# GLU before the attention, the SSM branch product beside the last pair of heads: one decoder layer on Trainium2

## The chip, the cores and the metric

One NeuronCore of a Trainium2 chip. The metric is the device time of one execution in microseconds. Engines as the profile names them: PE (TensorE matmul), PEld (its weight loads), DVE (VectorE), ACT (ScalarE), POOL (GpSimd), SP (SyncE, which issues most DMAs).

## The reference

One layer on 1040 positions (16 meta tokens and 1024 tokens) of width 1024, in float32:

```
xn = RMSNorm(h)
[q | k | v | u | gate_a | gate_b] = xn @ W_in
a  = stick-breaking attention(q, k, v)       (8 heads x 64, strictly causal)
y  = gelu(S5 state space model(u))           (512 channels)
s  = y * sigmoid(y @ W_glu + b)
h += (sigmoid(gate_a) * (a @ W_pa) + sigmoid(gate_b) * (s @ W_pb)) @ W_o
h += hierarchical MoE(RMSNorm(h))            (32 experts, two per token)
```

W_glu is 512 x 512, W_pa and W_pb are 512 x 1024. The change concerns s and the merge of the two branches.

## The kernel before

Every float32 product is made of three matmuls: both factors are split into a high and a low part (`split`, L101 on ACT and L102 on DVE) and `mm3` (L134 to L136) adds high x high, high x low and low x high in PSUM. Weights come through `load_w` (L150): a 512 KB tile `wr`, split into `wh` and `wl`, two buffers of each.

The stages, in the order of the source:

- Norms; the projection u; the SSM in four blocks of 128 channels (`ssm`), whose output goes to memory, `y_d` (L647). Beside it run the gates: 32 products `gt` with a sigmoid (L180), stored to `gate_d` (L181). 21 of them are woven into the SSM, 3 (`MF`) stand before the projections of the first heads, 8 beside the attention.
- The attention, in four pairs of heads. `att_proj` makes q, k and v of a pair (`qs`, `kh`, `kl`, `V`), `att_pair` its scores (L770, L771), their sigmoids (L773, L774, ACT), a mask (L776, POOL), a running product (L779, DVE), a product (L780, POOL), transposes (L794) and value products (L807, L812). Pairs 0 to 2 run beside the projections of the next pair, and their output goes to `attn_d` (L821). Pairs 0 and 2 use the buffers `aq0`, pairs 1 and 3 `aq1`.
- Beside pair 3, GLU: eight loads of y (L660) through two buffers, split into `yh` and `yl`; then for each of four blocks of 128 outputs and two halves of the tokens (`q`) twelve matmuls, a sigmoid (L681), a product with y (L682) and the split into `sh` and `sl`, which stay on chip. After it the attention output of pairs 0 to 2 is loaded and split into `ah` and `al` (L299); pair 3 writes its part there itself.
- The branch stage: for each of eight blocks `m` of 128 outputs and each half, twelve matmuls of the SSM branch (into `qk`), twelve of the attention branch (into `mm`), the two gates loaded (L347, L348), two products (L349, L353), a sum on POOL (L354) and the splits into the tiles `m` and `ms`. Gate tiles have two buffers each. The split of W_o runs beside it.
- The output projection, the router, the experts.

Tiles have fixed numbers of buffers, and a pool opened later takes the room of those closed before. `weave(main, fill, a, b)` sets the order in the source: b steps of `fill` evenly among a steps of `main`. A scheduler then puts the instructions of each engine into the order in which they become ready by its own estimates, earlier source first; on the chip each engine and SP run that order strictly.

```
weave(pair, chain(gl, loads()), 16, 18)   # before: GLU and the attn loads beside pair 3
```

Of the kernel before, what the change touches and what calls it, by code (L numbers as in the profile page):

```python
# [12 lines left out]
F32 = mybir.dt.float32  # L13
# [30 lines left out]
CL = (0, 512), (512, 768), (768, 1024)  # L44
SF, MF, GP = 21, 3, (3, 3, 2)
MQ = tuple((n, {'m': 6, 'ms': 2}[n]) for n in ('m', 'm', 'ms', 'm'))
MR = 6
CH3 = ((0, 352), (352, 696), (696, 1040))
CHV = ((0, 272), (272, 656), (656, 1040))
# [7 lines left out]
def weave(main, fill, n_main, n_fill):  # L57

    done = 0
    for k in range(n_main):  # L60
        next(main, None)
        while done * n_main < (k + 1) * n_fill:
            next(fill, None)
            done += 1


def drain(*gens):
    for g in gens:
        for _ in g:
            pass  # L70
# [3 lines left out]
def tile_block(ctx, tc, i, out):  # L74
# [3 lines left out]
    def pool(c, name, bufs=1, side=None, **kw):  # L78
        return c.enter_context(tc.tile_pool(name=name, bufs=bufs, side=side, reuse_waits="tile", **kw))
# [9 lines left out]
    u_d = dr.tile([512, T, NCH], F32, name="u_d")  # L89
    y_d = dr.tile([512, T, 128], F32, name="y_d")  # L90
    attn_d = dr.tile([512, S], F32, name="attn_d")
    gate_d = dr.tile([2 * D, S], F32, name="gate_d")
    h2_d = dr.tile([S, D], F32, name="h2_d")
    hg_d = dr.tile([S, D], F32, name="hg_d")
# [4 lines left out]
    def split(h, l, src, heng=None, leng=None):  # L99

        a = (A if heng is None else heng).copy(h, src)  # L101
        return a.ins, (V if leng is None else leng).tensor_sub(l, src, _f(h)).ins  # L102
# [29 lines left out]
    def mm3(ps, wh, wl, xh, xl, first, last):  # L132

        nc.tensor.matmul(ps, lhsT=wh, rhs=xh, start=first, stop=False)  # L134
        nc.tensor.matmul(ps, lhsT=wh, rhs=xl, start=False, stop=False)  # L135
        nc.tensor.matmul(ps, lhsT=wl, rhs=xh, start=False, stop=last)  # L136


    with ExitStack() as ca:
# [21 lines left out]
        with ExitStack() as cx:  # L161
# [102 lines left out]
            nc.sync.dma_start(tab_d.rearrange("(a p) w -> p a w", p=128), ei[:, None, :].to_broadcast([128, 8, 128]))  # L264


            con = pool(ctx, "con2")
            c3 = ExitStack()
            ap = pool(c3, "att", bufs=2)
# [1 line left out]
            cq = ExitStack()  # L271
            aq[0] = pool(cq, "aq0", bufs=2)
            st = {}
            drain(islice(gen, MF), att_proj(tc, ap, aq[0], ps, proj, ident, 0, st))
            for hp in range(3):
                pair = att_pair(tc, ap, ps, ident, hp, st, attn_d)
                fill = chain(att_proj(tc, ap, aq[(hp + 1) % 2], ps, proj, ident, hp + 1, st), islice(gen, GP[hp]))
# [9 lines left out]
        with ExitStack() as c4:  # L287
            c5 = ExitStack()
            p = pool(c5, "br", side="right")
            ah, al, sh, sl = (p.tile([128, 4, S], F32R, name=n) for n in ("ah", "al", "sh", "sl"))  # L290
            with ExitStack() as c6:
                nc.sync.dma_start(gb, i["glu_b"])
                at = pool(c6, "glu", bufs=2, side="right")
                gl = glu(tc, at, ps, i, load_w, mm3, split, gb, y_d, sh, sl)

                def loads():
                    for k in range(3):
                        a = wp.tile([128, 2, 512], F32, name="wr", bufs=2)
                        nc.sync.dma_start(a, attn_d[k * 128:k * 128 + 128])  # L299
                        split(ah[:, k], al[:, k], a.rearrange("p a b -> p (a b)"))  # L300
                        yield
                dst += ah, al
                weave(pair, chain(gl, loads()), 16, 18)
                drain(pair, gl)
            c3.close()
            con3 = pool(ctx, "con3")
            mp = pool(ctx, "mp")

            M = [[mp.tile([128, 4, 512], F32R, name=n, bufs=b).rearrange("p a (b c) -> p (a b) c", b=2) for _ in range(2)]
                 for n, b in MQ]  # L310
            wop = [pool(ctx, "wo0"), None]
            wo = i["w_out"].rearrange("(k p) c -> p k c", p=128)
            W = [None, None]

            def load_wo(hf):
                W[hf] = []
                for q in range(4):
                    if hf:
                        hl = [wop[1].tile([128, 2, 512], F32R, name="w1", bufs=8) for _ in range(2)]
                    else:  # L320
                        if q % 2 == 0:
                            pg = [wop[0].tile([128, 4, 512], F32R, name="w", bufs=4) for _ in range(2)]
                        hl = [x[:, q % 2 * 2:q % 2 * 2 + 2] for x in pg]
                    W[hf] += [[x[:, k] for x in hl] for k in range(2)]
                    r = wp.tile([128, 2, 512], F32, name="wr", bufs=2)
                    nc.sync.dma_start(r, wo[:, 2 * q:2 * q + 2, hf * 512:hf * 512 + 512])
                    split(*hl, r)
                    yield

            wa = i["w_branch_attn"].rearrange("(k p) c -> p k c", p=128)  # L330
            wb = i["w_branch_ssm"].rearrange("(k p) c -> p k c", p=128)
            w0 = load_wo(0)
            p = pool(c5, "gat", side="right", bufs=2)
            for m in range(KD):
                h, l = load_w([wb[:, :, m * 128:m * 128 + 128], wa[:, :, m * 128:m * 128 + 128]])
                T2 = []
                for q in range(2):
                    c = slice(q * 512, q * 512 + 512)
                    t = ps.tile([128, 512], F32, name="qk", bufs=2)
                    for k in range(4):  # L340
                        mm3(t, h[:, k, :], l[:, k, :], sh[:, k, c], sl[:, k, c], k == 0, k == 3)
                    T2.append(t)
                for q in range(2):
                    c = slice(q * 512, q * 512 + 512)
                    ga = p.tile([128, 512], F32, name="ga")
                    gb = p.tile([128, 512], F32, name="gb")
                    nc.sync.dma_start(gb, gate_d[D + m * 128:D + m * 128 + 128, c])  # L347
                    nc.sync.dma_start(ga, gate_d[m * 128:m * 128 + 128, c])  # L348
                    V.tensor_mul(gb, gb, T2[q])  # L349
                    t = ps.tile([128, 512], F32, name="mm", bufs=2)  # L350
                    for k in range(4):
                        mm3(t, h[:, 4 + k, :], l[:, 4 + k, :], ah[:, k, c], al[:, k, c], k == 0, k == 3)
                    V.tensor_mul(ga, ga, t)  # L353
                    P.tensor_add(ga, ga, gb)  # L354
                    for r in range(2):
                        mh, ml = M[2 * q + r]
                        split(mh[:, m], ml[:, m], ga[:, r * 256:r * 256 + 256])
                if m >= 2:
                    next(w0, None)
            c5.close()  # L360

            wop[1] = pool(ctx, "wo1")
            drain(load_wo(1))
            cw.close()
            rp = pool(ctx, "raw", side="right")
            rt = out_proj(tc, c4, pool, ps, i, ident, M, W, h2_d, hg_d, tab_d, rstd, bcast, con, con3, ei)
# [281 lines left out]
                                        ap=[[S, CH], [CH * S, 8], [1, 128]]), Y[ti * CH:ti * CH + CH])  # L648


def glu(tc, p, ps, i, load_w, mm3, split, gb, y_d, sh, sl):
    nc = tc.nc
    V, A, P = nc.vector, nc.scalar, nc.gpsimd
    yh = p.tile([128, 4, S], F32R, name="yh", bufs=1)
    yl = p.tile([128, 4, S], F32R, name="yl", bufs=1)
    yd = y_d.rearrange("f t c -> f (t c)")

    def load(k, q):
        y = p.tile([128, 512], F32, name="y", bufs=2)
        nc.sync.dma_start(y, yd[k * 128:k * 128 + 128, q * 512:q * 512 + 512])  # L660
        return y

    for k in range(4):
        for q in range(2):
            c = slice(q * 512, q * 512 + 512)
            split(yh[:, k, c], yl[:, k, c], load(k, q))
    yield
    wg = i["glu_w"].rearrange("(k p) c -> p k c", p=128)
    for m in range(4):
        h, l = load_w([wg[:, :, m * 128:m * 128 + 128]])  # L670
        for q in range(2):

            y = p.tile([128, 512], F32, name="y", bufs=2).rearrange("p (t c) -> p t c", t=T)
            nc.sync.dma_start(y, y_d[m * 128:m * 128 + 128, :, q * 64:q * 64 + 64])
            t = ps.tile([128, 512], F32, name="mm", bufs=2)
            y4 = [x.rearrange("p k (t c) -> p k t c", t=T)[:, :, :, q * 64:q * 64 + 64] for x in (yh, yl)]
            for k in range(4):
                mm3(t, h[:, k, :], l[:, k, :], y4[0][:, k], y4[1][:, k], k == 0, k == 3)

            sg = p.tile([128, 64, T], F32, name="sg", bufs=1)  # L680
            A.activation(sg, t.rearrange("p (t c) -> p c t", t=T), AF.Sigmoid, bias=gb[:, m:m + 1])  # L681
            V.tensor_mul(sg, sg, y.rearrange("p t c -> p c t"))  # L682
            c = slice(q * 512, q * 512 + 512)
            split(sh[:, m, c], sl[:, m, c], sg.rearrange("p c t -> p (c t)"))
            yield


# [772 lines left out]
```

## Time and profile before

| | |
|---|---|
| runs | 1500.51, 1498.16, 1494.89 us; median 1498.16 |
| profiled execution | 1493.12 us, span 1491.1 us, mean granted clock 0.983 |
| busy share of the span | PE 95%, PEld 77%, DVE 72%, ACT 54%, POOL 29% |
| stages, us from the start | SSM to about 265; attention to 634; branch stage to 704; output projection and router to 840; experts after that |

A line of a group tells the line of the source, the engine, the operation, what is written and read, the shape, the count, and behind the bar the busy time, the mean duration in ns, and the idle time of the engine before it with what ended it. "<-" in brackets names who was waited for.

### The profile page before, as it was taken

The numbers are of one execution on the slowest core, as the hardware profiler recorded it, in microseconds if no ns is written. First come the engines' busy times: TensorE is split into PE (matmuls) and PEld (weight loads), VectorE is DVE, ScalarE is ACT, GpSimd is POOL, SyncE is SP. The second block draws the span as 40 slices with busy tenths as digits, with TensorE's granted clock in tenths as the row PEclk, the third lists the DMA queues.
The fourth block names the chain that finished last, engine by engine and source line by source line (L and its number), as shares of the span: only waits on it lengthen the run. The fifth ranks groups of instructions, "written<-read, shape, count | busy, mean of one in ns | idle before, by whom it ended". The sixth has DMA issues, their size and how long they took to land. (4 is left out here: it accounts for less than half of the span.)

```text
span 1491.1 us, 19767 instructions
## 1 busy us (share of the span) xinstructions
PE 1410.5 (95%) x7028; PEld 1144.0 (77%) x7028; DVE 1079.5 (72%) x1590; ACT 798.1 (54%) x1173; POOL 425.3 (29%) x372
## 2 busy tenths in 40 slices
PE   7989899999999979999999699999999999999994
PEld 5977788998989967778788477777777777777762
DVE  5799986465757577575476687777777777777757
ACT  6222222465656576431222277777777777777743
POOL 2162411134444464332255421111111111111033
PEclk9999999999999999999999799999999999999998
DMA  8233443211111114254863499999999999999753
GB/s 257 73 86 88 99 114 87 57 46 58 35 48 36 29 57 131 81 184 149 299 249 109 182 369 376 372 370 357 370 376 368 372 377 368 368 378 367 309 214 152
DMA packets 131749, 313.87 MB, mean 210 GB/s; under 512 B 27889, under 2 KB 81777, under 8 KB 107074
## 3 DMA queue, kind: packets, MB, share of 16 engines
q1 hardware_dynamic: 120450, 295.07, 55.3%
q0 software_dynamic: 9728, 16.83, 3.0%
q8 instruction: 56, 0.92, 0.2%
q10 hardware_dynamic: 1472, 0.69, 0.2%
q14 instruction: 43, 0.35, 0.1%
HBM read 284.03 MB, written 44.11 MB: 220 GB/s over the span
## 5 line engine op out<-in xcount | busy, mean ns | idle before, releaser
L136 PE MATMUL mm<-xh,wl 128*128 128x512 f32 (+4 forms) x608 | 220.3, 362 | 5.4 <-DVE wl L102 5.4
L134 PE MATMUL mm<-xh,wh 128*128 128x512 f32 (+4 forms) x608 | 220.7, 363 | 1.7 <-DVE kl L710 0.7
L135 PE MATMUL mm<-xl,wh 128*128 128x512 f32 (+4 forms) x608 | 220.1, 362 | 0.5 <-DVE xl L225 0.5
L136 PEld LDWEIGHTS mm<-xh,wl 128*128 128x128 f32 x608 | 114.5, 188 | 19.8 <-DVE wl L102 6.6
L134 PEld LDWEIGHTS mm<-xh,wh 128*128 128x128 f32 x608 | 114.2, 188 | 16.1 <-PE mm L136 1.6
L135 PEld LDWEIGHTS mm<-xl,wh 128*128 128x128 f32 x608 | 114.3, 188 | 13.5 <-DVE xl L225 1.0
L779 DVE TENSOR_TENSOR_SCAN pr<-pr 128x144 f32<-128x144 f32 (+3 forms) x64 | 91.2, 1426 | 42.1 <-POOL pr L776 40.8
L1174 POOL DMA_INDIRECT ye_d<-w,tab x32 | 33.3, 1041 | 270.9 <-ACT w L1167 270.3
L1090 DVE TENSOR_TENSOR w<-r,w 128x2048 fp32r<-128x2048 f32 x39 | 92.7, 2377 | 16.2 <-ACT w L1089 16.2
L1090 DVE TENSOR_TENSOR w<-m,w 128x2048 fp32r<-128x2048 f32 x40 | 90.8, 2284 | 16.7 <-ACT w L1089 16.7
L1096 POOL DMA_INDIRECT w<-hg_d,tab x31 | 40.7, 1314 | 207.1 <-PE tr L1117 205.8
L780 POOL TENSOR_TENSOR be<-be,pr 128x143 f32<-128x143 f32 (+3 forms) x64 | 86.7, 1359 | 38.9 <-DVE pr L779 36.6
L102 DVE TENSOR_TENSOR xl<-tr,xh 128x512 fp32r<-128x512 f32 x64 | 43.8, 686 | 57.9 <-ACT xh L101 57.9
L101 ACT CAST xh<-tr 128x512 fp32r<-128x512 f32 x64 | 37.5, 588 | 77.7 <-PE tr L1117 73.8
L102 DVE TENSOR_TENSOR wl<-wr,wh 128x1024 fp32r<-128x1024 f32 (+1 forms) x44 | 59.1, 1343 | 27.6 <-ACT wh L101 27.5
L1089 ACT CAST w<-r 128x2048 fp32r<-128x2048 f32 x40 | 76.3, 1908 | 3.8 <-PE mm L893 3.1
L1130 PE MATMUL a<-w,xh 128*128 128x512 f32 x196 | 77.8, 397 | 0.0
L101 ACT CAST wh<-wr 128x1024 fp32r<-128x1024 f32 (+1 forms) x44 | 44.5, 1011 | 61.8 <-PE mm L135 40.6
L1089 ACT CAST w<-m 128x2048 fp32r<-128x2048 f32 x40 | 76.5, 1912 | 0.8
L1132 PE MATMUL a<-w,xl 128*128 128x512 f32 x196 | 76.6, 391 | 0.0
L1131 PE MATMUL a<-w,xh 128*128 128x512 f32 x196 | 76.4, 390 | 0.0
L1167 ACT ACTIVATE w<-o,tab 128x512 f32<-128x512 f32 x64 | 44.2, 690 | 53.1 <-PE o L1160 53.1
(557 smaller groups left out, 3934.3 us busy)
## 6 DMA issues: line engine op xcount, KB each, us to landing
r<-in_w_dram SPq DMA_DIRECT2D x96, 1024.0 KB, 8.8
m<-in_w_dram SPq DMA_DIRECT2D x96, 1024.0 KB, 8.9
wr<-in_w_in_dram SPq DMA_DIRECT2D x32, 512.0 KB, 4.3
gate_d<-gt SPq DMA_DIRECT2D x32, 256.0 KB, 2.2
m<-ye_d SPq DMA_DIRECT2D x12, 512.0 KB, 8.6
x<-in_x_dram SPq DMA_DIRECT2D x8, 512.0 KB, 4.7
y<-y_d SPq DMA_DIRECT2D x16, 256.0 KB, 3.1
wr<-in_w_out_dram SPq DMA_DIRECT2D x8, 512.0 KB, 4.5
```

What stands on the lines that cost most here:

```text
L101: a = (A if heng is None else heng).copy(h, src)
L102: return a.ins, (V if leng is None else leng).tensor_sub(l, src, _f(h)).ins
L134: nc.tensor.matmul(ps, lhsT=wh, rhs=xh, start=first, stop=False)
L135: nc.tensor.matmul(ps, lhsT=wh, rhs=xl, start=False, stop=False)
L136: nc.tensor.matmul(ps, lhsT=wl, rhs=xh, start=False, stop=last)
L779: V.tensor_tensor_scan(rv, rv, rv, 1.0, op0=OP.mult, op1=OP.bypass)
L780: P.tensor_mul(be[:, :W - 1], be[:, :W - 1], pr[:, 1:W])
L1089: A.copy(h, raws[n])
L1090: low = lambda: (P if other else V).tensor_sub(l, raws[n], _f(h))
L1130: nc.tensor.matmul(acc[e][w], lhsT=xh[:, kk], rhs=h[:, k], start=(kk == 0), stop=False)
L1131: nc.tensor.matmul(acc[e][w], lhsT=xh[:, kk], rhs=l[:, k], start=False, stop=False)
L1132: nc.tensor.matmul(acc[e][w], lhsT=xl[:, kk], rhs=h[:, k], start=False, stop=(kk == KD - 1))
```

## The change

GLU becomes a stage of its own after the SSM, with the three `MF` gates after its first step (the loads and splits of y), and before the attention's buffers are opened. Its result goes to memory, `s_d`, and is not split there. Beside pair 3 a new generator `early` loads s and splits it, and makes for the first six (`AHEAD`) of the eight blocks m the SSM branch product, multiplies it with its gate and stores it over the gate in memory; after each of the first three blocks it loads a part of the attention output. The branch stage then has only the attention product for these six blocks and loads the finished SSM part in place of the gate; the last two blocks are as before. Branch weights of one matrix are now loaded for two blocks at a time.

```diff
+AHEAD = 6
+    s_d = dr.tile([512, S], F32, name="s_d")
...
+            with ExitStack() as c6:
+                nc.sync.dma_start(gb, i["glu_b"])
+                gl = glu(tc, pool(c6, "glu", bufs=2, side="right"), ps, i, load_w, mm3, split, gb, y_d, s_d)
+                next(gl)
+                drain(islice(gen, MF), gl)
+
             con = pool(ctx, "con2")
...
-            drain(islice(gen, MF), att_proj(tc, ap, aq[0], ps, proj, ident, 0, st))
+            drain(att_proj(tc, ap, aq[0], ps, proj, ident, 0, st))
...
             ah, al, sh, sl = (p.tile([128, 4, S], F32R, name=n) for n in ("ah", "al", "sh", "sl"))
-            with ExitStack() as c6:
-                nc.sync.dma_start(gb, i["glu_b"])
-                at = pool(c6, "glu", bufs=2, side="right")
-                gl = glu(tc, at, ps, i, load_w, mm3, split, gb, y_d, sh, sl)
-
-                def loads():
-                    for k in range(3):
-                        a = wp.tile([128, 2, 512], F32, name="wr", bufs=2)
-                        nc.sync.dma_start(a, attn_d[k * 128:k * 128 + 128])
-                        split(ah[:, k], al[:, k], a.rearrange("p a b -> p (a b)"))
-                        yield
-                dst += ah, al
-                weave(pair, chain(gl, loads()), 16, 18)
-                drain(pair, gl)
+            p = pool(c5, "gat", side="right", bufs=2)
+            wa, wb = (i[n].rearrange("(k p) c -> p k c", p=128) for n in ("w_branch_attn", "w_branch_ssm"))
+
+            def load_s(src, h, l, k):
+                a = wp.tile([128, 2, 512], F32, name="wr", bufs=2)
+                nc.sync.dma_start(a, src[k * 128:k * 128 + 128])
+                split(h[:, k], l[:, k], a.rearrange("p a b -> p (a b)"))
+
+            def branch(m, q, h, l, h_, l_, name):
+                c = slice(q * 512, q * 512 + 512)
+                t = ps.tile([128, 512], F32, name=name, bufs=2)
+                for k in range(4):
+                    mm3(t, h[:, k], l[:, k], h_[:, k, c], l_[:, k, c], k == 0, k == 3)
+                return t
+
+            def gate(row, m, q):
+                g = p.tile([128, 512], F32, name="ga" if row else "gb")
+                d = gate_d[row * D + m * 128:row * D + m * 128 + 128, q * 512:q * 512 + 512]
+                nc.sync.dma_start(g, d)
+                return g, d
+
+            def early():
+                for k in range(4):
+                    load_s(s_d, sh, sl, k)
+                yield
+                for m in range(AHEAD):
+                    if m % 2 == 0:
+                        w = load_w([wb[:, :, (m + n) * 128:(m + n) * 128 + 128] for n in range(2)])
+                    for q in range(2):
+                        g, d = gate(1, m, q)
+                        V.tensor_mul(g, g, branch(m, q, *(x[:, m % 2 * 4:m % 2 * 4 + 4] for x in w), sh, sl, "mm"))
+                        nc.sync.dma_start(d, g)
                         yield
+                    if m < 3:
+                        load_s(attn_d, ah, al, m)
+
+            dst += ah, al
+            fill = early()
+            weave(pair, fill, 14, 1 + 2 * AHEAD)
+            drain(pair, fill)
...
             for m in range(KD):
-                h, l = load_w([wb[:, :, m * 128:m * 128 + 128], wa[:, :, m * 128:m * 128 + 128]])
-                T2 = []
+                if m >= AHEAD:
+                    w = load_w([x[:, :, m * 128:m * 128 + 128] for x in (wb, wa)])
+                    at = 4
+                    T2 = [branch(m, q, *(x[:, :4] for x in w), sh, sl, "qk") for q in range(2)]
+                else:
+                    at = m % 2 * 4
+                    if not at:
+                        w = load_w([wa[:, :, (m + n) * 128:(m + n) * 128 + 128] for n in range(2)])
                 for q in range(2):
...
+                    (g_, _), (ga, _) = gate(1, m, q), gate(0, m, q)
+                    if m >= AHEAD:
+                        V.tensor_mul(g_, g_, T2[q])
+                    V.tensor_mul(ga, ga, branch(m, q, *(x[:, at:at + 4] for x in w), ah, al, "mm"))
+                    P.tensor_add(ga, ga, g_)
...
-def glu(tc, p, ps, i, load_w, mm3, split, gb, y_d, sh, sl):
+def glu(tc, p, ps, i, load_w, mm3, split, gb, y_d, s_d):
...
-            sg = p.tile([128, 64, T], F32, name="sg", bufs=1)
+            sg = p.tile([128, 64, T], F32, name="sg", bufs=2)
             A.activation(sg, t.rearrange("p (t c) -> p c t", t=T), AF.Sigmoid, bias=gb[:, m:m + 1])
             V.tensor_mul(sg, sg, y.rearrange("p t c -> p c t"))
-            c = slice(q * 512, q * 512 + 512)
-            split(sh[:, m, c], sl[:, m, c], sg.rearrange("p c t -> p (c t)"))
+            nc.sync.dma_start(s_d[m * 128:m * 128 + 128, q * 512:q * 512 + 512], sg.rearrange("p c t -> p (c t)"))
```

## Rows read from the trace of the kernel before

**Rows 1.** The page, busy us, share of the span, instructions.

```profile
PE 1410.5 (95%) x7028; PEld 1144.0 (77%) x7028; DVE 1079.5 (72%) x1590; ACT 798.1 (54%) x1173; POOL 425.3 (29%) x372
```

**Rows 2.** Timeline of PE, 258.5 to 266: start, duration, instruction.

```profile
259.02 0.39 PE L136 MATMUL mm<-xh,wl 128*128 128x512 f32 x1
...
265.27 0.39 PE L136 MATMUL mm<-xh,wl 128*128 128x512 f32 x1
```

**Rows 3.** Timeline of PE, 544.9 to 549.

```profile
545.79 0.28 PE L812 MATMUL pv<-wth,V 128*128 128x256 f32 x1
545.91 0.28 PE L812 MATMUL pv<-wtl,V 128*128 128x256 f32 x1
...
546.14 0.31 PE L812 MATMUL pv<-wtl,V 128*128 128x128 f32 x1
```

**Rows 4.** Groups of PE instructions, 520 to 704.

```profile
L134 PE MATMUL qk<-sh,wh 128*128 128x512 f32 x64 | 25.3, 395 | 1.6 <-DVE gb L349 1.6
L134 PE MATMUL mm<-ah,wh 128*128 128x512 f32 x60 | 23.8, 397 | 2.1 <-ACT sg L681 0.9 <-DVE ga L353 0.8 <-ACT ah L825 0.5
...
L807 PE MATMUL pv<-wth,V 128*128 128x256 f32 (+1 forms) x96 | 22.5, 366 | 0.9 <-DVE ao L820 0.5 <-ACT wth L801 0.4
L794 PE MATMUL tr<-ident,be 128*128 128x128 f32 x127 | 22.4, 291 | 1.9 <-POOL be L780 1.8
L770 PE MATMUL qk<-kh,qs 128*128 128x392 f32 (+8 forms) x36 | 14.1, 394 | 1.2 <-ACT be L774 1.0
...
L134 PE MATMUL mm<-yh,wh 128*128 128x512 f32 x32 | 12.9, 425 | 0.5 <-ACT yh L101 0.5
...
L812 PE MATMUL pv<-wtl,V 128*128 128x256 f32 (+1 forms) x24 | 6.8, 309 | 2.8 <-DVE wtl L804 2.8
```

**Rows 5.** Windows: length, busy us of PE, PEld, DVE, ACT, POOL, granted clock, DMA share, GB/s.

```profile
520.00:545.00 25.00, 19.26 (x122) 16.29 (x120) 17.40 (x22) 16.91 (x42) 18.25 (x21) 0.93 0.18 52
520.00:704.00 184.00, 168.21 (x822) 137.83 (x821) 121.56 (x144) 89.64 (x196) 76.56 (x74) 0.98 0.40 122
```

**Rows 6.** GLU's y loads and splits: ns min/median/max, first and last start; landing us.

```profile
L660 SPq DMA_DIRECT2D y<-y_d x8: 319/320/537, 538.7 to 568.2; - x8
...
DMA to landing us min/median/max: 2.7/2.8/3.1
...
L101 ACT CAST yh<-y x8: 617/620/674, 548.3 to 571.2; 128x512 fp32r<-128x512 f32 x8
L102 DVE TENSOR_TENSOR yl<-y,yh x8: 659/806/2445, 550.9 to 571.8; 128x512 fp32r<-128x512 f32 x8
```

**Rows 7.** Line 180 up to 262 us.

```profile
L180 ACT ACTIVATE gt<-mm x24: 585/594/605, 79.5 to 258.8; 128x512 f32<-128x512 f32 x24
```

**Rows 8.** Line 647, stores of y, and their landing.

```profile
L647 SPq DMA_DIRECT2D y_d<-Y x32: 303/432/1443, 166.0 to 264.7; - x32
...
DMA to landing us min/median/max: 1.9/2.4/4.1
```

**Rows 9.** Windows, an idle stretch in the SSM stage.

```profile
100.00:120.00 20.00, 12.40 (x53) 9.15 (x52) 19.83 (x11) 3.77 (x6) 10.86 (x4) 0.83 0.17 53
```

**Rows 10.** GLU's product with y, by its tile.

```profile
L682 DVE TENSOR_TENSOR sg<-sg,y x8: 1067/1096/1622, 574.5 to 608.3; 128x512 f32<-128x512 f32 x8
```

**Rows 11.** Waits, 240 to 300: waiting line, releaser, us in total, times, longest.

```profile
POOL V L729 <- DMA y_d<-Y: 16.3, 1, 16.3
```

**Rows 12.** Timeline of all engines, 684.2 to 692, one gate buffer; landing of line 348.

```profile
684.30 0.68 DVE L353 TENSOR_TENSOR ga<-ga,mm 128x512 f32<-128x512 f32 x1
...
685.15 1.29 POOL L354 TENSOR_TENSOR ga<-ga,gb 128x512 f32<-128x512 f32 x1 [4.47 <-DVE ga L353]
...
687.85 0.42 DVE L102 TENSOR_TENSOR m<-ga,m 128x256 fp32r<-128x256 f32 x1
...
688.30 0.32 SPq L348 DMA_DIRECT2D ga<-gate_d  x1
...
DMA to landing us min/median/max: 2.7/3.6/6.0
```

More of the change, by code (lines that the diff above doesn't have):

```diff
@@ L328, in load_wo @@
                     yield
-            wa = i["w_branch_attn"].rearrange("(k p) c -> p k c", p=128)
-            wb = i["w_branch_ssm"].rearrange("(k p) c -> p k c", p=128)
             w0 = load_wo(0)
-            p = pool(c5, "gat", side="right", bufs=2)
             for m in range(KD):
-                h, l = load_w([wb[:, :, m * 128:m * 128 + 128], wa[:, :, m * 128:m * 128 + 128]])
-                T2 = []
-                for q in range(2):
-                    c = slice(q * 512, q * 512 + 512)
[L339 to L354, printed above, removed]
+                if m >= AHEAD:
[6 more added lines that the diff above has]
+                        w = load_w([wa[:, :, (m + n) * 128:(m + n) * 128 + 128] for n in range(2)])
+                for q in range(2):
+                    (g_, _), (ga, _) = gate(1, m, q), gate(0, m, q)
[3 more added lines that the diff above has]
+                    P.tensor_add(ga, ga, g_)
                     for r in range(2):
@@ L678, in glu @@
                 mm3(t, h[:, k, :], l[:, k, :], y4[0][:, k], y4[1][:, k], k == 0, k == 3)
-            sg = p.tile([128, 64, T], F32, name="sg", bufs=1)
+            sg = p.tile([128, 64, T], F32, name="sg", bufs=2)
             A.activation(sg, t.rearrange("p (t c) -> p c t", t=T), AF.Sigmoid, bias=gb[:, m:m + 1])
             V.tensor_mul(sg, sg, y.rearrange("p t c -> p c t"))
-            c = slice(q * 512, q * 512 + 512)
-            split(sh[:, m, c], sl[:, m, c], sg.rearrange("p c t -> p (c t)"))
+            nc.sync.dma_start(s_d[m * 128:m * 128 + 128, q * 512:q * 512 + 512], sg.rearrange("p c t -> p (c t)"))
             yield
```

## The prediction, made before the changed kernel was run

> **What bounds the kernel now.** I read the page first: PE is busy 1410.5 of 1491.1 us [rows 1], so every matmul counts wherever it is put, and the change keeps their number. A move can only change the time in which PE has nothing to issue. So I looked for that time where the change acts: the windows view and the groups of PE's instructions for 520 to 704 us, from the last projections to the end of the branch products.
>
> Busy time misleads there. Matmuls overlap: one of 512 columns is listed with 0.39 us, but from 259.02 to 265.27 PE starts 27 of them, 0.23 apart [rows 2], and the 256-column products of attention start 0.12 apart [rows 3]. I therefore count. In 520 to 704 there are 64 lots of three for the SSM branch (192), 179 for the attention branch, 96 for GLU and 9 of projections: 476 by 0.2315 is 110.2 us [rows 4]. The transposes (127, and 3 of the projections) and the value products (96 and twice 24) are 274 by 0.12, 32 us. The score products, 36 and as many of the low part, lie between 0.12 and 0.23 by width; 72 by 0.16 is 11.5 us [rows 4]. Work is 154 of 184 us: 30 us without issue. The busy column would say 184 - 168 = 16 [rows 5]. The Trainium skill's "Perfetto Trace Analysis", section "Identifying the Most-Contended Engine", says that matmul busy time is no good measure because matmuls are pipelined; by the busy column the stretch could give back 16 us at most and the sum below would come out at least 12 us higher, while the starts in this trace side with the page.
>
> Of the 30 us, about 9 lie in 520 to 545 (122 short matmuls by some 0.13 is 16 of 25 us [rows 5]), most of the rest up to 640: pair 3 has only GLU beside it, and GLU's inputs come late. Its y loads go out from 538.7 and its first copy runs at 548.3 [rows 6].
>
> **The change, part by part.** *GLU moved ahead of the attention.* Its 96 matmuls (22.2 us) leave the late stretch and go between the last SSM output and pair 0's projections. What covers it there? The three gate products beside it in the source are no cover: all 24 gate tiles given out up to this point are done by 258.8 already, inside the SSM stage [rows 7]. In the kernel before, pair 0's projections follow at once (the products of 259.02 to 265.27 [rows 2]). After the change GLU needs y of the last block: its stores are issued until 264.7 and land 2.4 later, at 267 [rows 8]. Then eight y tiles go through two buffers: load 2.8, copy 0.62, subtraction 0.66 [rows 6], some 0.3 of hand-over, 4.4 us a pair. Three rounds and a last one with its second tile, 4.7: 267 + 13.2 + 4.7 = 285. In between only the first two steps can run three of their four parts (18 matmuls, 4.2 us). The other 78 take 18.0 us: 303.
>
> Two smaller costs come on top. The clock: in 100 to 120, where PE was busy 12.4 of 20 us, the granted clock averages 0.83: some 7 us at 1.2 GHz in place of 2.4, 0.17 x 20 = 3.4 us lost [rows 9]. GLU follows a gap, so I put 2 us into it (0 to 3.4). And each result waits for its second y load, its product with y (1.1 us [rows 10]) and now a store, through two buffers; 1 to 3 us at the start, I take 1. PE leaves GLU at about 306 (304 to 310). Pair 0's projections begin there instead of at 258.5, where the last gates end: 47.5 us later (45 to 52), 22.2 of them moved work and 25 new idle time.
>
> Can those projections run beside GLU instead? I think not. V of pair 0 shares its room with the SSM's last output: its clearing waited 16.3 us for the y store [rows 11]. GLU shares its room with the projections of the even pairs: y lay in memory from 541.5, the first copy into yh ran only at 548.3 [rows 6], after the last value product of pair 2 at 546.14 [rows 3]. In the change GLU's pool lies in this stretch again, so pair 0's projections would have to wait until GLU has read yh. The same rows make me expect that its y loads for the first three blocks do not go ahead of the last block's store.
>
> *Branch product beside pair 3.* 144 matmuls (33.3 us) replace GLU's 96 there. Their inputs lie in memory long before; sh and sl take the room of xh and xl, free after the last projection at about 521, not that of pair 2. Four loads of 512 KB, their splits and a weight block give a start near 540 to 546, so the 9 us of 520 to 545 stay. From there 33 us of branch and about 28 of pair 3 (the 44 us of attention counted above less the 16 done by 545) fill some 65 us; I leave 4 idle (2 to 14, since a product that waits for its PSUM tile holds pair 3's scores behind it on PE), and 2 at the seam.
>
> New on SP: 8 stores of s, 4 loads of it, and for 12 products a gate load and a store, each waiting for its DVE product, with the next gate load, the attn loads and the next weights behind it on SP. Twelve rounds through two buffers of load 3.6, product 0.7 [rows 12] and a store, at 2.4 like that of y [rows 8], are 40 us, inside pair 3's 65: no cost; without that cover they would cost 40 - 33 = 7. Splits are the same elements, only later. The extra 10 MB or so of transfers I cost at nothing: the DMA engines are busy 0.40 of 520 to 704 [rows 5].
>
> *Branch stage.* For m under 6 only the attention half is left, 12 matmuls a half row: 2.8 us. Its gate buffer is held from the product at 684.30 over POOL's addition and the last split to the reload at 688.30, 4.0, and the load lands 3.6 after [rows 12]: 7.6 for two buffers, 3.8 a half row. Before, 24 matmuls (5.6 us) hid that; now DVE's input is late by 1.0 twelve times, 12 us, less the first loads, which are early: I take 9 (0 if they run ahead, 14 if SP delays them).
>
> **Sum.** Late stretch: 154 - 22.2 + 9 + 4 + 2 + 9 = 156 instead of 184, 28 less. Early: 47.5 more. **+19 us**. With the bounds: from 45 - 40 = +5 (idle 9, 2, 0, 1) to 52 - 12 = +40 (idle 9, 14, 3, 14). The profiled execution took 1493.12, 5.0 less than the median of the runs, 1498.16; I set the 19 on the median: **1517**.
>
> **Rivals.** *GLU is covered* (ends on the other side). If pair 0's projections, 11 us for q and as much or more for k and v, do run in the gap of 258.5 to 285, GLU costs its 22.2 us of work alone: 22.2 - 28 = -6, and -18 at the low end of the late idle time; 1480 to 1492, faster from the point where over 20 of the 25 us are filled. For it: those products need nothing of GLU and took no pause before. Against it: the shared room. 0.18, two thirds of it faster by over 0.5%.
>
> *The y loads run early.* If the loads of blocks 0 to 2 do not wait for Y's room, only two tiles are left at 267, and GLU starts in full at 272 instead of 285: +6, 1504. 0.12. The Trainium skill's "DMA: Bandwidth & Descriptors", section "Measured (HBM→SBUF, 128 partitions, SWDGE, issued from GpSimd)", lists 341 GB/s at 1 MB; an estimate by it puts all 2 MB of y at 6 us, and the sum at +7. The rows show 2.8 us for 256 KB and two buffers, so here the ring sets the pace and not the rate.
>
> *The change does not do what it says.* If the loads of s and the branch weights sit on SP behind attn stores that wait for pair 2, or the gate ring holds PE, the product is not beside pair 3 but after it: the late idle time stays near 30 and the price is 47.5 - 22.2 = +25 to +33, 1523 to 1531. 0.15.
>
> **How the numbers follow.** The forecast, +5 to +40 with +19 likeliest, has 0.55; covered GLU 0.18; early y 0.12; no filling 0.15. Half a percent is 7.5 us, about what a measurement of this kernel can tell from no change. Faster: two thirds of 0.18, 0.12. Same: the rest of it, two thirds of early y and a twentieth from the forecast's low end, 0.18. Slower: 0.70. The range leaves out most of the covered case and the far end: 1497 to 1534.
>
> **What would show it.** Right: PE without work, but for a few GLU products, from about 259 to 285 with the granted clock at half; the first qs copy near 310 instead of 263.6; y loads in pairs 4.4 apart after the last y store; branch products of sh from about 540 between pair 3's products; gate reloads 3.8 apart in the branch stage. Wrong: projection products between 259 and 300 beside GLU's, or y loads before 260, or a late stretch with over 30 us idle.

## The result and the profile after

The changed kernel takes 1534.2 us, median of four runs (1531.05 to 1535.93), against 1497.85 for the kernel before beside them: ratio 1.0238, interval 1.0224 to 1.0253. That is 36 us slower; forecast were 19, with 1497 to 1534 as the range, so the time lies at its far end. The two profiled executions that are compared below lie 41 us apart, since the one of the kernel before was 5 us faster than its median.

The page of the changed kernel, busy time by engine, answers to [rows 1]:

```profile
PE 1424.7 (93%) x7028; PEld 1153.0 (75%) x7028; DVE 1078.5 (70%) x1586; ACT 798.8 (52%) x1169; POOL 420.4 (27%) x372
```

Again 7028 matmuls: the 41.2 us by which the profiled span grew (1491.1 to 1532.3) are time in which PE had nothing to issue, or ran at half clock (granted clock 0.76 and 0.73 in the first two windows below). The windows of the changed kernel (columns as in [rows 5]), the GLU stage first, then from the last projection to pair 3's last output and from there to the first output product:

```profile
255.00:270.00 15.00, 3.29 (x15) 2.32 (x13) 3.98 (x8) 4.10 (x7) 0.00 (x0) 0.76 0.38 105
270.00:285.00 15.00, 9.42 (x24) 5.50 (x24) 4.71 (x8) 3.94 (x7) 0.00 (x0) 0.73 0.37 115
285.00:310.00 25.00, 24.51 (x103) 19.44 (x102) 12.54 (x13) 8.99 (x13) 0.04 (x1) 0.97 0.89 236
...
567.50:682.20 114.70, 99.50 (x521) 85.83 (x519) 65.95 (x68) 60.08 (x136) 54.97 (x60) 0.93 0.39 127
682.20:746.10 63.90, 52.05 (x208) 40.13 (x209) 35.05 (x54) 17.16 (x36) 19.64 (x14) 0.95 0.51 169
```

The same two late stretches of the kernel before:

```profile
522.20:633.80 111.60, 98.88 (x521) 81.72 (x520) 76.56 (x79) 68.55 (x155) 55.70 (x60) 0.97 0.31 90
633.80:707.00 73.20, 70.14 (x303) 56.67 (x304) 45.49 (x66) 20.36 (x40) 21.65 (x14) 1.00 0.52 169
```

Fifteen matmuls in the first window, 24 in the second, 103 in the third: PE stands empty for y, then half empty. The stretch beside pair 3 holds 521 matmuls before and after, and is 3 us longer instead of shorter. The lots of three there, by the groups of PE's instructions in these two stretches, before and then after:

```profile
L134 PE MATMUL mm<-yh,wh 128*128 128x512 f32 x32 | 12.9, 425 | 0.5 <-ACT yh L101 0.5
...
L134 PE MATMUL qk<-sh,wh 128*128 128x512 f32 x16 | 6.5, 406 | 0.0
```

```profile
L136 PE MATMUL mm<-sh,wh 128*128 128x512 f32 x48 | 18.9, 395 | 0.0
```

The kernel before already ran 48 products of the SSM branch (16 by 3) beside the end of pair 3, besides GLU's 96. So the 144 early products do not put more work there than stood there; they replace these 144. The prediction counted GLU's 96 alone. The branch stage has lost 95 matmuls and only 9.3 us. The first `qs` copy came at 309.07 (263.6 before), the last projection at 567.5 (522.2): 45.3 us later. The late stretch is 178.6 instead of 184.8, 6.2 back; what follows it is 2.1 longer. 45.3 - 6.2 + 2.1 = 41.2.

Because busy time misleads for PE, I split each stretch into work and idle time: every matmul is charged the distance to the next start that its kind keeps while PE waits for nothing (0.227 us for 512 columns, 0.118 for 256, 0.108 for a transpose, the score products by their width), and the rest, half clock included, is idle. One kind keeps another distance: pair 3's value products of 256 columns, which take `wth` unsplit, one product in place of two, start 0.215 apart. Eight of them without a wait, before and then after (the last one's own 0.38 us leaves 1.51 for seven distances):

```profile
611.79 1.89 PE L807 MATMUL pv<-wth,V 128*128 128x256 f32 x8
```

```profile
663.87 1.89 PE L831 MATMUL pv<-wth,V 128*128 128x256 f32 x8
```

Pair 3 has 96 of these products (16 of them with 128 columns). Charged like the value products of the other pairs they would count 8.4 us too few, and those would look like idle time.

| us: length = work + idle | last projection to pair 3's last output | from there to the output projection | both |
|---|---|---|---|
| before | 111.6 = 90.3 + 21.7 | 73.2 = 68.8 + 4.0 | 184.8 |
| after | 114.7 = 90.3 + 24.8 | 63.9 = 47.2 + 16.5 | 178.6 |

(The rest of a few tenths is rounding and the matmul at the cut.) Predicted for both: 132 of work and 24 idle, 156 us. Work is 137.5; idle time is 41.3. The late stretch is 23 us longer than predicted: 5.5 of work and 17 of idle time. Half clock is a small part of it: beside pair 3 the granted clock is 0.93, which makes some 16 us at 1.2 GHz, and PE issued about 6 us of work in them, so that they cost some 6 us (some 3 in the kernel before, at 0.97).

### The profile page after: what moved, and what is told of

Read it like the earlier page. It is cut to its first block, busy times and chain, and to the rows that moved or that the text cites. A ratio compares the mean times of both kernels' runs of the same rounds, so it can differ in the third digit from the quotient of the medians.

```text
span 1532.3 us, 19824 instructions
## 1 busy us (share of the span) xinstructions
PE 1424.7 (93%) x7028; PEld 1153.0 (75%) x7028; DVE 1078.5 (70%) x1586; ACT 798.8 (52%) x1169; POOL 420.4 (27%) x372
## 5 line engine op out<-in xcount | busy, mean ns | idle before, releaser
L136 PEld LDWEIGHTS mm<-xh,wh 128*128 128x128 f32 x608 | 114.4, 188 | 16.4 <-PE mm L138 1.7
L104 DVE TENSOR_TENSOR wl<-wr,wh 128x1024 fp32r<-128x1024 f32 (+1 forms) x44 | 55.1, 1253 | 33.7 <-ACT wh L103 33.4
L797 ACT ACTIVATE pr<-qk 128x144 f32<-128x144 f32 (+6 forms) x112 | 52.1, 465 | 42.5 <-PE qk L795 28.0
```

## The experiments

### What is the GLU stage's price, and can it be covered?

**Eight y buffers**, in both places where `glu` makes `y`:

```diff
-        y = p.tile([128, 512], F32, name="y", bufs=2)
+        y = p.tile([128, 512], F32, name="y", bufs=8)
```

> GLU's y tiles have eight buffers in place of two; six of them lie beside the SSM's last output buffer, not in it. Theory (the gap in front of GLU is the two-buffer ring that starts only after the last y store): loads of blocks 0 to 2 go out before 265, GLU runs in full from about 271 in place of 284, and the time falls by 10 to 13: 1521 to 1524. Rival (the wait for the last block alone sets GLU's start; the ring is hidden behind it): under 4 us, 1530 to 1536.

Measured: 1527.17 us, ratio 1.021 (1.0193 to 1.0227), faster than the changed kernel by 4 us by the ratios and 7 by the medians, between the theory's 1521 to 1524 and the rival's 1530 to 1536. The y loads by their line, of the changed kernel:

```profile
L685 SPq DMA_DIRECT2D y<-y_d x8: 319/320/427, 266.0 to 279.2; - x8
...
DMA to landing us min/median/max: 2.8/2.8/3.0
```

and with eight buffers:

```profile
L685 SPq DMA_DIRECT2D y<-y_d x8: 338/428/433, 264.4 to 268.8; - x8
...
DMA to landing us min/median/max: 2.8/2.8/2.8
```

Each load lands after 2.8 us either way. With two buffers the eight go out over 13.2 us, with eight over 4.4, and `qs` starts 4.8 earlier (304.3). So the ring (the two buffers used in turn) costs 4 to 7 us, and the rest stays: no load went out before 264.4, when the last y stores had been issued, though the theory had those of blocks 0 to 2 ahead of them.

**Gates as cover.** Three of the gate products that stand beside pairs 0 to 2 are put behind `next(gl)`:

```diff
-SF, MF, GP = 21, 3, (3, 3, 2)
+SF, MF, GP = 21, 6, (2, 2, 1)
```

> Three of the gate products that run beside pairs 0 to 2 stand in the GLU stage instead (MF 6, GP 2,2,1): 3 x 24 matmuls x 0.2315 = 16.7 us of PE work, put into the 13 us in which PE waits for y. Theory (PE is the limit beside pairs 0 to 2, where the changed kernel idles 7.6 us in 259, so work taken out there shortens it one for one, and the GLU stage's wait hides it): GLU starts about 4 later, the last projection ends about 13 earlier, 1518 to 1525 us. Rival (the pairs need these products as cover for their own chain of scores, scans and transposes): the pairs idle that much more and the time stays at 1530 to 1536.

Measured: 1539.89, ratio 1.0266 (1.0242 to 1.029), 4 us slower than the changed kernel by the ratios, whose intervals overlap. The theory's 1518 to 1525 fell; the rival's reason held, though the time lies above its 1530 to 1536. The wait of PE for y in the GLU stage, in the changed kernel and then with the gates moved (engine, line, who was waited for: total us, times, longest):

```profile
PE mm L136 <- ACT yh L103: 17.3, 4, 11.7
```

```profile
PE mm L136 <- ACT yh L103: 3.5, 2, 2.1
```

PE's waits from 310 to 570, with the gates moved (the first 9 us are still GLU stage):

```profile
PE mm L136 <- ACT wh L103: 2.6, 4, 0.9
PE mm L138 <- DVE wl L104: 2.5, 4, 0.7
PE mm L136 <- DVE kl L734: 2.0, 2, 1.2
PE mm L136 <- DVE qs L725: 1.6, 2, 1.0
```

and of the changed kernel:

```profile
PE mm L138 <- DVE wl L104: 0.8, 2, 0.5
PE mm L136 <- DVE kl L734: 0.7, 1, 0.7
PE tr L756 <- ACT vf L744: 0.6, 1, 0.6
PE mm L136 <- DVE qs L725: 0.5, 1, 0.5
```

The cover is real: the GLU stage's idle time falls from 23.6 to 16.5. But beside pairs 0 to 2 idle time rises from 7.6 to 20.7, some 8 of these 13 us in many small waits for split weights and for evictions of the projections. So work could not be taken out of this stretch one for one, though 97% of it was work. The waits point to what the gate products had hidden there, the weight splits and the evictions; that is not shown apart from the order, since `weave` spreads fewer steps with fewer gates, and some 40 attention matmuls slid behind the last projection.

### Are the early branch products worth anything?

**No early products.** All eight blocks as in the kernel before; GLU stays early, s and the attention output are loaded beside pair 3.

```diff
-AHEAD = 6
+AHEAD = 0
...
+                for m in range(3):
+                    load_s(attn_d, ah, al, m)
+                    yield
...
-                    if m < 3:
-                        load_s(attn_d, ah, al, m)
...
-            weave(pair, fill, 14, 1 + 2 * AHEAD)
+            weave(pair, fill, 14, 4)
```

> GLU stays a stage of its own, but no branch product is made beside pair 3 (AHEAD 0); all eight blocks make theirs in the branch stage, as in the kernel before. Theory (the early products take away what covered the end of pair 3, and their gate ring stretches pair 3): pair 3 runs bare, some 60 us in place of the 83 between its first and last running product after the change, its end is again covered by SSM branch products, and the kernel is 10 to 25 us faster than after the change: 1510 to 1524. Rival (the early products do fill idle time of PE, and the whole loss is the gap in front of GLU): without them 144 matmuls of 0.23, 33 us, lose their cover: 1555 to 1567.

Measured: 1526.79, ratio 1.0202 (1.0183 to 1.022). Without them the kernel is 5 to 7 us faster, just above the theory's 1510 to 1524 and far from the rival's 1555 to 1567. Both stretches answer (windows of this run, cut as above):

```profile
568.40:667.80 99.40, 82.46 (x425) 69.38 (x423) 56.79 (x56) 56.56 (x132) 50.52 (x60) 0.88 0.21 67
667.80:741.00 73.20, 70.21 (x304) 56.70 (x305) 45.41 (x66) 20.44 (x41) 21.69 (x15) 1.00 0.54 169
```

Pair 3 ends after 99.4 us; with 96 matmuls more beside it (21.8 us: the 144 early ones, less the 48 of the SSM branch that stand beside its end without them) it takes 114.7, 15.3 more. In the branch stage the same products cost 73.2 - 63.9 = 9.3.

### Where does the branch stage idle?

Three runs. **W_o later** (`next(w0, None)` from m = 4 instead of 2) and **the two whole blocks first**:

```diff
-                if m >= 2:
+                if m >= 4:
```

> The first load of W_o goes out with branch block 4 in place of block 2. After the change SP stood from 667.8 to 685.7 before a branch weight load, because both weight tiles held parts of W_o whose split waited for pair 3's end at 682; the gate loads stood behind it. Theory (PE's restart after pair 3 waits on that queue): PE's idle time of 680 to 710, some 15 us, falls by 5 to 12: 1522 to 1529. Rival (the restart waits on the attention output alone): no change, 1531 to 1536.

```diff
-            for m in range(KD):
+            for n_m, m in enumerate((6, 7, 0, 1, 2, 3, 4, 5)):
...
-                if m >= 2:
+                if n_m >= 2:
```

> The branch stage takes blocks 6 and 7, whose SSM products are not made early, first. Theory (the end of pair 3 stands bare because no product without attention is left): 48 matmuls of 0.23, 11 us, run beside the last steps of pair 3, in the 22 us in which PE was idle between 663 and 700: 6 to 11 us faster than after the change, 1523 to 1528. Rival (those weights sit on SP behind waiting loads as well, or pair 3's steps are what PE waits for in any order): under 3 us, 1531 to 1536.

Measured: 1534.47 (1.0252, 1.0235 to 1.0269) and 1533.24 (1.025, 1.023 to 1.0269), both no change. The first did not do what it was made for. SP's own instructions in the changed kernel at the seam, where PE starts again after pair 3's last output:

```profile
667.52 0.32 SPq L317 DMA_DIRECT2D ga<-gate_d  x1
685.67 0.38 SPq L152 DMA_DIRECT2D wr<-in_w_branch_attn_dram  x1
...
687.90 0.38 SPq L360 DMA_DIRECT2D wr<-in_w_out_dram  x1
688.33 0.94 SPq L317 DMA_DIRECT2D gb<-gate_d  x2
```

and with W_o later:

```profile
657.66 0.43 SPq L360 DMA_DIRECT2D wr<-in_w_out_dram  x1
659.84 11.55 SPq L317 DMA_DIRECT2D ga<-gate_d  x2
689.74 0.38 SPq L360 DMA_DIRECT2D wr<-in_w_out_dram  x1
691.17 0.32 SPq L317 DMA_DIRECT2D gb<-gate_d  x1
```

SP stands from 667.8 to 685.7 in the one, from 671.4 to 689.7 in the other, before a load that needs a `wr` buffer, and the gate loads queue behind it: only the load that waits was exchanged. The order of blocks moved some 5 us of idle time from pair 3's end into the branch stage: pair 3's stretch takes 6.1 us more for 10.7 more of work. So these two leave the seam itself open.

**Four gate buffers:**

```diff
-            p = pool(c5, "gat", side="right", bufs=2)
+            p = pool(c5, "gat", side="right", bufs=4)
```

> Four buffers for each gate tile instead of two, nothing else. Theory A (the chain from gate load to freed buffer is longer than two steps of the product, both beside pair 3, 4.3 us a step against 2.8 of work, and in the branch stage): the idle time of the branch stage falls from 15 to about 5, pair 3 ends up to 4 earlier, 1519 to 1527 us. Theory B (the restart after pair 3 waits for the weight load behind the W_o parts, and the rest of pair 3 is its own chain): at most 3 gained, 1531 to 1535.

Measured: 1526.99, ratio 1.0189 (1.0167 to 1.0211), 7 us faster than the changed kernel. The waits of PE in the branch stage, of the changed kernel and then of this run:

```profile
PE mm L136 <- DVE gb L378: 11.1, 5, 7.0
```

```profile
PE mm L136 <- DVE gb L378: 5.8, 2, 5.5
```

The five waits for a gate become two, and the stretch 53.5 us instead of 63.9, with 2.3 less work in it. What is left is one long wait, 5.5 at the seam. But pair 3's stretch is no shorter (116.2): the gate ring was the price in the branch stage, not beside pair 3.

### Is pair 2's tail the cause?

In the changed kernel the splits of s stand in pair 2's last steps. POOL's products there, by its timeline:

```profile
576.26 6.04 POOL L804 TENSOR_TENSOR be<-be,pr 128x783 f32<-128x783 f32 x2
...
587.89 4.94 POOL L804 TENSOR_TENSOR be<-be,pr 128x1039 f32<-128x1039 f32 x2 [3.62 <-DVE pr L803]
```

The kernel before has the last of these lines at 537.04 with 2.55 us. **Order:** the splits of s, weights and attention output are queued behind the first step of pair 3, by its last sigmoid `a0` and its last running product `v0`:

```diff
-                for k in range(4):
-                    load_s(s_d, sh, sl, k)
+                a0, v0 = st["a"], st["v"]
+                with tc.issue_after(a0), tc.issue_after(v0):
+                    for k in range(4):
+                        load_s(s_d, sh, sl, k)
...
```

> The splits of s, of the first branch weights and of the attention output are queued, on ACT and on VectorE, behind the first step of pair 3 (its last sigmoid and its last running product), where the kernel before had the splits of y. Nothing else changes. Theory (these splits stand in pair 2's tail: between the last projection and pair 2's last POOL product there are 25 us against 17 in the kernel before, with the POOL products at 2.8 to 4.5 us instead of 1.6 to 2.2): pair 2 and the head of pair 3 are 5 to 9 shorter, and since pair 3 is set by its own chain the end moves by most of it: 1525 to 1530 us. Rival (the early products then start later by as much and the gate ring after them sets the end): pair 3's first output comes earlier, its last does not, 1532 to 1536.

Measured: 1531.33, ratio 1.0236 (1.0222 to 1.0251): no change. The same products in this run:

```profile
574.62 1.57 POOL L808 TENSOR_TENSOR be<-be,pr 128x783 f32<-128x783 f32 x1
...
578.74 1.80 POOL L808 TENSOR_TENSOR be<-be,pr 128x911 f32<-128x911 f32 x1 [2.06 <-DVE pr L807]
...
583.52 2.55 POOL L808 TENSOR_TENSOR be<-be,pr 128x1039 f32<-128x1039 f32 x2
```

The mechanism was there and went (pair 2's last long product starts 14.6 us after the last projection instead of 20.4), and the time did not follow: the splits now stand in pair 3's head, whose first output comes 38.7 after the last projection, as before the edit (38.6). My theory of this run fell, and the rival's sign, an earlier first output, did not come either.

### What does a product beside pair 3 cost?

Two runs with order and eight y buffers: with early products and four gate buffers, and without early products. The first is the changed kernel with the order above and

```diff
-            p = pool(c5, "gat", side="right", bufs=2)
+            p = pool(c5, "gat", side="right", bufs=4)
...
-        y = p.tile([128, 512], F32, name="y", bufs=2)
+        y = p.tile([128, 512], F32, name="y", bufs=8)
```

> The order of the splits, four buffers for each gate tile (7 faster alone) and eight y buffers (7 faster alone) together. Theory (three costs in three stretches): 1534 - 7 - 7 - 7 = 1513, 1510 to 1517 us; the stretch from the last projection to the output projection then is some 162 against 185 before and 179 after. Rival (order and gate buffers free the same time, since pair 3's chain limits both): 1518 to 1522.

Measured: 1519.17, ratio 1.0145 (1.0127 to 1.0163), the best of all, 14 us under the changed kernel. The three edits alone sum to 4 + 7 + 0 by the ratios. The theory's 1510 to 1517 was missed; the time is in the rival's 1518 to 1522.

The second has these y buffers and the order, two gate buffers, and, with the loads as in the first run without early products,

```diff
-AHEAD = 6
+AHEAD = 0
...
```

> No early branch products (AHEAD 0), the order of the splits and eight y buffers. Theory (the splits in pair 2's tail cost 5 to 9 with and without early products): 1527 - 7 - 7 = 1513, 1510 to 1516 us. Against the run with early products and four gate buffers it shows what the early products are worth once both costs are gone: by the sum of the prediction 22 of work less what pair 3 is stretched, so that run should be 5 or more faster; if the two are equal, products beside pair 3 are paid for there one for one.

Measured: 1520.72, ratio 1.0158 (1.0144 to 1.0172): the same as the first within the intervals, and not the theory's 1510 to 1516. Early products gain nothing even with their buffers. The last run adds PE work alone to this one: twelve groups of branch products beside pair 3 that nobody reads, with the whole branch stage kept. One pair of weight blocks is loaded and split for them, and `weave` spreads 13 steps in place of 4.

```diff
...
+                for m in range(6):
+                    for q in range(2):
+                        branch(m, q, *(x[:, m % 2 * 4:m % 2 * 4 + 4] for x in w), sh, sl, "mm")
+                        yield
...
-            weave(pair, fill, 14, 1 + 2 * AHEAD)
+            weave(pair, fill, 14, 13)
```

> The run with order, eight y buffers and no early products (1520.7), and beside pair 3 twelve groups of twelve branch matmuls into the buffers mm that nobody reads: 144 x 0.2315 = 33.3 us of PE work with no gate load, no VectorE product and no store; one pair of weight blocks is loaded for it. The branch stage stays whole, so the work is added, not moved. In the run without it, PE idles 37 us between the last projection and pair 3's last output. Theory (PE runs its queue in order and pair 3 is a chain of steps that each pass through PE, so that every product put between them delays the chain, and the idle time stays): most of the 33 is paid, 1542 to 1554 us. Rival (the products fit into the idle time, and what stretched pair 3 in the changed kernel were their gate loads, VectorE products and stores): 1521 to 1530.

Measured: 1539.81, ratio 1.0285 (1.0259 to 1.0312), 19 us more than without. The windows of pair 3's stretch and the branch stage, without the added products (cut 2 us later than in the table):

```profile
562.70:659.90 97.20, 80.45 (x428) 67.05 (x426) 59.62 (x59) 58.31 (x137) 52.10 (x60) 0.91 0.21 68
659.90:731.60 71.70, 69.33 (x301) 56.11 (x302) 44.37 (x64) 18.34 (x38) 21.63 (x14) 1.00 0.54 173
```

and with them:

```profile
563.50:684.30 120.80, 110.87 (x572) 92.50 (x570) 58.22 (x60) 59.94 (x138) 57.55 (x60) 0.96 0.19 59
684.30:758.20 73.90, 70.69 (x301) 57.38 (x302) 44.32 (x64) 18.40 (x38) 21.63 (x15) 0.98 0.52 168
```

DVE, ACT and DMA do much the same as without (59.6 and 58.2, 58.3 and 59.9 us, share 0.21 and 0.19), PE has 144 matmuls more, and the stretch is 23.6 us longer. Idle time was there, 27.1 us of it, and only 9 were filled. The theory's 1542 was not quite reached, the rival's 1530 is far off. By the whole time the price is lower than by the stretch, 19 us for 32.5 of work: in the profiled execution with the added products, what follows the branch stage is 5 us shorter (783.1 against 788.1), which the edit does not explain.

| beside pair 3 | length = work + idle | branch stage |
|---|---|---|
| GLU late (before) | 111.6 = 90.3 + 21.7 | 73.2 |
| none, 2 y buffers | 99.4 = 68.5 + 31.2 | 73.2 |
| early products (after) | 114.7 = 90.3 + 24.8 | 63.9 |
| none, order, 8 y buffers | 95.2 = 68.5 + 27.1 | 73.7 |
| early, order, 8 y and 4 gate buffers | 116.2 = 92.1 + 24.2 | 53.4 |
| PE work alone, order, 8 y buffers | 118.8 = 101.0 + 18.0 | 75.9 |

Work put beside pair 3 costs 15.3 for 21.8 (after), 21.0 for 23.6 (four gate buffers), 23.6 for 32.5 (PE alone): 0.7 to 0.9 us for each us, and 0.6 by the order of blocks (6.1 for 10.7) and by the whole time of PE alone. Taken out, work returns somewhat less: GLU's 21.8 returned 12.2 to 16.4, 0.6 to 0.75.

### Both halves mended at once

Six early blocks with four gate buffers, and none with two, both without the order and with

```diff
-SF, MF, GP = 21, 3, (3, 3, 2)
+SF, MF, GP = 21, 6, (2, 2, 1)
...
-        y = p.tile([128, 512], F32, name="y", bufs=2)
+        y = p.tile([128, 512], F32, name="y", bufs=8)
```

> The three edits together: eight y buffers (7 faster alone), three more gate products in the GLU stage, four buffers for each gate tile. If the costs lie in different stretches, as the idle times of the trace say, they add up: 1534 - 7 - 13 - 10 = 1504, 1499 to 1510 us. If the eight y buffers and the moved gates fill the same wait, the two give 13 to 16 and not 20, 1506 to 1514. If the pairs need their gates: 1514 to 1522. Not under the kernel before in any of these.

> No early branch products (AHEAD 0, as in the first experiment, 1526.8), with eight y buffers and the three gates in the GLU stage. Theory (GLU stage and late stretch are separate): 1527 - 7 - 13 = 1507, 1503 to 1512 us, so that against the run with four gate buffers and six early blocks it is decided whether early products gain once their buffers suffice: they do if that run is over 3 faster than this one. Rival (the pairs need their gates): 1518 to 1524.

Measured: 1524.55 (1.018, 1.0162 to 1.0197) and 1523.14 (1.0177, 1.0148 to 1.0205). Both miss their sums as the gates alone do: beside pairs 0 to 2 the idle time is about 21 and 19 us. The second lies in its rival's 1518 to 1524, the first above all its ranges. And they are equal within the intervals, as the pair of runs above. No version beat the kernel before.

## Why the prediction was right, and where its sum was not

**Direction and range.** Right: slower, by a stage that costs more early than it gives back late. Two terms, +47.5 and -28, were set against each other; the first was right (45.3), the second over four times too large (6.2 came back), and outside its own bounds of 12 to 40. That the time still lies at the end of the range is luck: the +40 there was the worst of both terms, and the early one came out at the low end of its 45 to 52. The prediction's own sign of being wrong, a late stretch with over 30 us idle, came too: it is 41.

**GLU stage, +47.5 (45 to 52): measured 45.3.** Step by step: last y store issued at 263.7 (264.7), first load 265.95 (267), pairs of loads 4.1 to 4.4 apart (4.4), GLU over at 303.1 (303 before the two small costs, which came to nothing more). The copies show the ring, on ACT's timeline of the changed kernel:

```profile
268.68 1.28 ACT L103 CAST yh<-y 128x512 fp32r<-128x512 f32 x2 [8.95 <-DMA y<-y_d]
272.94 1.27 ACT L103 CAST yh<-y 128x512 fp32r<-128x512 f32 x2 [2.99 <-DMA y<-y_d]
...
309.07 0.58 ACT L724 CAST qs<-mm 64x512 fp32r<-64x512 f32 x1 [2.10 <-PE mm L138]
```

**The rivals.** GLU covered by pair 0's projections: none ran before 303. Early y loads: none before the last block's store, and even eight buffers gave 5 of that rival's 13 us. "Does not do what it says" had the late idle time near 30 and 1523 to 1531; the idle time was 41, though the product did stand beside pair 3, from 587.9 (540 to 546 plus the 45 us shift was predicted), with its gate loads some 4 us apart.

**The step that failed** is this one: "33 us of branch and about 28 of pair 3 fill some 65 us; I leave 4 idle", and 2 at the seam. It is short in two ways. First, "the 256-column products of attention start 0.12 apart" was read from rows 3, which are value products of pair 2, and was charged to pair 3's as well. Those start 0.215 apart, so that pair 3's share was 8.4 us too small and as much idle time was seen that was work: the late stretch before had 25.7 us of it, not 30. (The other distances were taken a little too long, so that the sum of work was only 5 short.) Second, it treats the idle time beside pair 3 as room. From the last projection to pair 3's last output, 24.8 us were idle where 15 were predicted (9 + 4 + 2). The run with PE work alone shows that idle time there is mostly not room: of 27.1 us, 32.5 us of added work filled 9, with no gate loads, VectorE products or stores of its own. Why, is argued and not shown: PE takes its matmuls in the order that the scheduler wrote, and pair 3 is a chain of scores, sigmoids, mask, running product, transposes and value products that passes through PE several times a step, so a group of twelve matmuls (2.8 us) ahead of a transpose delays all that follows, while the waits between stay. Whether smaller groups at other places would fill more, no run shows.

The same exchange applies to what was taken out: GLU's work had been paid for beside pair 3, but at 0.6 to 0.75, and not at 1 as "154 - 22.2" has it.

**Branch stage, 9 idle (0 to 14): measured 16.5.** The mechanism, two gate buffers under half the product, is shown by the run with four, which took it to 8.2. The term was short by the seam: one wait of 7.0 for a product with a gate (`gb`) whose load stood on SP behind a weight load, priced at 2. That this queue is the cause is not shown: with four buffers a wait of 5.5 stayed, and the run made to shorten the queue did not shorten it.

**By the waits.** In the late stretch of the changed kernel the longest waits of PE, behind the 11.1 us for the gates shown above, are:

```profile
PE tr L818 <- POOL be L804: 6.9, 2, 4.9
PE pv L836 <- ACT pr L797: 2.8, 1, 2.8
PE pv L836 <- ACT be L798: 2.7, 1, 2.7
```

These are waits in the pairs' own chain; there is none for sh or sl, and 0.2 us for a weight: the early product's inputs were in time, as predicted.

## What to carry to other kernels

Idle time of PE beside a latency chain that itself runs through PE is not room: measure what a filler costs there (the same stretch with and without it) before counting on it; here it was 0.6 to 0.9 us for each us. Before counting idle time at all, read the distance of starts for each kind of matmul in the stretch itself: two kinds of one width differed by a factor of 1.8 here. Work that leaves such a stretch returned 0.6 to 0.75 us for each us here, and it needs a new place that has cover: a stage that reads through memory what the stage before has just written has none of its own. And where a product is halved, its operand ring must be re-checked: two buffers that sufficed for 24 matmuls did not for 12.

## What was not expected of the hardware

POOL's products of two tiles took up to twice their time while VectorE's splits from and to on-chip memory ran: 128 x 1039 with its short follower 4.94 us instead of 2.55, and 2.55 again once the splits stood elsewhere. VectorE's timeline of the changed kernel has two splits in these 4.94 us (from 587.89):

```profile
588.01 1.19 DVE L104 TENSOR_TENSOR wl<-wr,wh 128x1024 fp32r<-128x1024 f32 x1
...
589.33 1.20 DVE L104 TENSOR_TENSOR al<-wr,ah 128x1024 fp32r<-128x1024 f32 x1
```

Together they take 2.39 us, as much as the products lost. The Trainium skill's "SBUF — State Buffer", section "SBUF: two separate sides", says that a VectorE instruction with two inputs in this memory and a GpSimd instruction that reads it share one pair of ports, which the one that starts first holds to its end; the lines agree. That the time did not move when it was gone was the second surprise.
